# HGRN2 levels 4 and 8 from one set of keys: four 192-column matmuls in place of eight of 64 columns, and one yield fewer

## The chip, the cores and the metric

The kernel runs on one core of a Trainium2 chip. The metric is device microseconds of one execution; the kernel before takes 2802.47 us (median of 3 runs, 2801.3 to 2804.57). TensorE is PE in the rows below, VectorE is DVE, ScalarE is ACT and SyncE (which issues the DMAs) is SP.

## What is computed

One step of one decoder layer, for a prompt of 16 meta tokens and 256 tokens and for 8 single sample tokens, in float32:

```
x <- LN1(alpha*x + 0.5*SwiGLU_1(x))
x <- LN2(alpha*x + Mixer(x))        # retention (8 heads of 256) and HGRN2 (16 heads of 128)
x <- LN3(alpha*x + 0.5*SwiGLU_2(x))
```

In the mixer one projection `x @ w_in` gives ten parts of 2048 columns. The change lies in HGRN2, whose chunk is

```
b = cumsum(logf);  decay[i,j] = exp(b[i] - b[j]) for j <= i, else 0
A = einsum('bhid,bhjd,bhijd->bhij', q, k, decay)
o = A @ v + (q * exp(b)) @ S;   S_new = exp(b_last) * S + (k * exp(b_last - b))^T @ v
```

and every head's output is divided by the root of its mean square (`head_rms_norm`) before the gates.

## The kernel before, in words

**Dense stream.** All weights come as units of 512 KB, 8 blocks of 128x128. For each unit SP issues one load into `raw` (L158), ACT rounds it into `whi` (L161) and DVE subtracts to get the rest `wlo` (L162). `raw`, `whi` and `wlo` have three buffers each, so ACT can start `whi` of unit n only when PE has done its last matmul of unit n-3. PE multiplies each block three times (L191: `whi` by `xh`, `whi` by `xl`, `wlo` by `xh`), 24 matmuls per unit. I count units from the kernel's start, and "396.0" is the place on PE ahead of the first matmul of unit 396.

**Mixer.** Two column chunks are projected at a time, 16 k-steps each, so 4 k-steps use up one unit. After each k-step `pump` lets every waiting thread count down; a thread that has counted out runs on to its next `yield n` and then counts n k-steps. There are two kinds of thread: `mix_ret` (one for each of 8 retention heads) and `mix_hg` (one for each of 8 pairs u = 0 to 7 of HGRN2 heads). So PE's order is written by hand: the threads' small matmuls stand between dense matmuls, at a place that the sums of the yields decide. The other engines' order comes from a scheduler, in which the weight loads have high priority; it is fixed when the kernel is built, and each engine takes its instructions strictly in that order.

**mix_hg.** The decayed scores of a 128-token block are built by levels s = 1, 2, 4, ..., 64. At level s, `Q` holds queries with the decay since the start of their s-chunk, `K` keys with the decay to the end of theirs. Scores between an odd chunk's queries and the even chunk's keys ahead of it go into a PSUM bank `pl` (levels 4, 8 and 16 with L698: for each of two heads and two blocks all 128 keys by the block's 64 odd queries). DVE copies what a mask selects into `acch` (L734), multiplies the even keys and odd queries by their chunk's factor (L205 `K`, L205 `Q`) and yields 6 k-steps (8 after level 1). Levels 1 and 2 come from sums of products over the partitions (L202). After the levels, for each head h: transposes of K (`ptk`, L745), the sample states (`smh`: load L752, ACT L754, DVE L755), the state (`pst`), the sample queries (`pq`, L776), the output (`po`, L785 and L786). Then the square of `po` is split into `hhi` (ACT, L196) and `hlo` (DVE, L197), and 7 k-steps later PE adds it up over the partitions, `pv` (L202, once with `hhi` and once with `hlo`). `mix_ret` has the same kind of sum, `pvr` with `rhi` and `rlo`, its own scores `psc` (L848), states `psr` (L864), sample queries `pqr` (L894), and DVE updates of the sample states, `smr` (L885).

Banks of all these small groups (`mx_bank`) rotate through four.

Of the kernel before, what the change touches and what calls it, by code (L numbers as in the profile page):

```python
# [10 lines left out]
F32 = mybir.dt.float32  # L11
F32R = mybir.dt.float32r
U8 = mybir.dt.uint8
AF = mybir.ActivationFunctionType
ALU = mybir.AluOpType
# [3 lines left out]
P = 128  # L19
# [4 lines left out]
NMETA, SEQ, NS = 16, 256, 8  # L24
# [17 lines left out]
LEVELS = (1, 2, 4, 8, 16, 32, 64)  # L42
MASKED = 5

MASKS = {1: [0], 2: [1, MASKED], 4: [2], 8: [3], 16: [4]}
W_LEVEL = 6


# [53 lines left out]
def trunk(ctx: ExitStack, tc: tile.TileContext, A, O):  # L102
    nc = tc.nc
    cst = ctx.enter_context(tc.tile_pool(name="cst", bufs=1))
# [11 lines left out]
    def mx_bank(name):  # L116
        return ps_m.tile([P, 512], F32, tag="mx", name=name)
# [10 lines left out]
    lb = cst.tile([P, KC], F32, tag="lb", name="lb")  # L128
    olb = cst.tile([P, KC], F32, tag="olb", name="olb")
    dec = cst.tile([P, 3, HR], F32, tag="dec", name="dec")  # L130
    msk = cst.tile([P, MASKED + 1, 2 * P], U8, tag="msk", name="msk")
    lnb = cst.tile([P, 2, 2, KC], F32R, tag="lnb", name="lnb")
    nc.vector.memset(ones, 1.0)
    nc.scalar.copy(ones_r, ones)
# [69 lines left out]
    def mul(out, a, b):  # L204
        nc.vector.tensor_tensor(out=out, in0=a, in1=b, op=ALU.mult)  # L205
# [4 lines left out]
    def sub(out, a, b):  # L210
        nc.vector.tensor_tensor(out=out, in0=a, in1=b, op=ALU.subtract)
# [17 lines left out]
    def x_tiles(c, which, n=T):  # L229
        for e, (x, nm) in enumerate(((xh, "xh"), (xl, "xl"))):  # L230
            o = 4 * ((2 * c + e) // 8 % 2) + 8 * (c % 2) * e
            x[c] = xp.tile([P, XP], F32R, tag=f"{nm}{c}", name=f"{nm}{which}_{c}")[:, o : o + n]
# [206 lines left out]
    with tc.tile_pool(name="inp", bufs=2) as ip:  # L439
        def tokens(queue, c0, c1):  # L440
            x0 = ip.tile([P, c1 - c0, T], F32, tag=f"x0{c0}", name=f"x0{c0}", bufs=1)
            queue.dma_start(x0, A["x"][:, c0:c1, :])
            for c in range(c0, c1):
                x_tiles(c, 0)
                split(xh[c], xl[c], x0[:, c - c0, :])


        pw = mx_bank("pw")
        for _ in range(WARM):
            nc.tensor.matmul(pw[:, :P], ones, ones, start=True, stop=True)  # L450
        for c in range(2):
            with turn(2 * c):
                tokens(nc.scalar, c, c + 1)
        for c in range(2, KC, 2):
            with turn(c + 1):
                tokens(nc.sync, c, c + 2)
        mf = ip.tile([P, MASKED + 1, 2 * P], F32, tag="mf", name="mf", bufs=1)
        nc.sync.dma_start(mf[:, :MASKED, :], A["msk"])

        even = ip.tile([P, 1], F32, tag="even", name="even", bufs=1)  # L460
        nc.vector.tensor_reduce(out=even, in_=mf[:, 0, :], op=ALU.max, axis=mybir.AxisListType.X)
        nc.vector.tensor_copy(mf[:, MASKED, :], mf[:, 1, :])
        nc.vector.tensor_scalar(out=mf[:, 1, :], in0=mf[:, 1, :], scalar1=even, scalar2=None, op0=ALU.mult)
        sub(mf[:, MASKED, :], mf[:, MASKED, :], mf[:, 1, :])
        nc.vector.tensor_copy(msk, mf)
    nc.sync.dma_start(lnp, A["lnp"])
    nc.sync.dma_start(lbt, A["lb"])
# [7 lines left out]
    with tc.tile_pool(name="yp", bufs=1) as yp:  # L475
        yh, yl = [None] * KC, [None] * KC
        with tc.tile_pool(name="mp", bufs=1) as mp:
# [7 lines left out]
            def tmp(name, shape=(P, T), bufs=1, dt=F32, tag=None):  # L485
                if name in rows:
                    rows[name] = rows[name][1:] + rows[name][:1]
                    return rp.tile(list(shape), dt, tag=rows[name][-1], name=name)
                return mp.tile(list(shape), dt, tag=tag or name, name=name, bufs=bufs)
# [148 lines left out]
            def mix_hg(u, f, k, q, v):  # L638

                Q = tmp("Q", (P, 2, SEQ))  # L640
                K = tmp("K", (P, 2, LP))
# [8 lines left out]
                acc = tmp("acch", (P, 2 * SEQ))  # L650
# [11 lines left out]
                for h in range(2):  # L662
# [12 lines left out]
                    out=acc.rearrange("p (b c) -> p b c", b=4), in0=pd.rearrange("p (b c) -> p b c", b=4),  # L675
                    in1=ident.unsqueeze(1).to_broadcast([P, 4, P]), op=ALU.mult)
                Tt = f
                for s in LEVELS:
                    pl = mx_bank("pl")
                    if s == 1:  # L680
                        sums(pl[:, :SEQ], hilo, 2)
                    elif s == 2:
                        sums(pl.rearrange("p (i c) -> p i c", i=2), hilo)
                    for h in range(2 if s > 2 else 0):
                        for b in range(2):
                            k0, q0, o = NMETA + b * P, b * P, (2 * h + b) * min(s, 64)
                            if s == 64:
                                nc.tensor.matmul(
                                    pl[0:s, o : o + s], K[:, h, k0 : k0 + s], Q[:, h, q0 + s : q0 + 2 * s],
                                    start=True, stop=True)  # L690
                            elif s == 32:
                                for j in (0, 64):
                                    nc.tensor.matmul(
                                        pl[j : j + s, o : o + s], K[:, h, k0 + j : k0 + j + s],
                                        Q[:, h, q0 + j + s : q0 + j + 2 * s], start=True, stop=True, tile_position=(0, j))
                            else:
                                o = (2 * h + b) * 64
                                nc.tensor.matmul(  # L698
                                    pl[:, o : o + 64], K[:, h, k0 : k0 + P],
                                    Q[:, h, q0 : q0 + P].rearrange("p (n t s) -> p n t s", t=2, s=s)[:, :, 1, :],  # L700
                                    start=True, stop=True)

                    if s == NMETA:
                        Tt = Tt[:, :, 1:]
                    k0 = 0 if s < NMETA else NMETA
                    n = LP - k0
                    nb = n // s
                    m = nb // 2
                    t2 = Tt[:, :, :nb].rearrange("p h (n t) -> p h n t", t=2)
                    kv = K[:, :, k0:].rearrange("p h (n t s) -> p h n t s", t=2, s=s)  # L710
                    qv = Q.rearrange("p h (n t s) -> p h n t s", t=2, s=s)
                    mq = SEQ // (2 * s)
                    mul(kv[:, :, :, 0, :], kv[:, :, :, 0, :], t2[:, :, :, 1].unsqueeze(3).to_broadcast([P, 2, m, s]))
                    mul(qv[:, :, :, 1, :], qv[:, :, :, 1, :], t2[:, :, m - mq :, 0].unsqueeze(3).to_broadcast([P, 2, mq, s]))
                    Tn = tmp(f"T{2 * s}", (P, 2, m))
                    mul(Tn, t2[:, :, :, 0], t2[:, :, :, 1])
                    Tt = Tn
                    if s == 1:

                        q4 = Q.rearrange("p h (n t i) -> p h n t i", t=2, i=2)[:, :, :, 1, :]  # L720
                        hilo = [tmp("prod" + t, (P, 2, SEQ), dt=F32R, tag=t) for t in ("smh", "vbh")]
                        for j in range(2):
                            pr = tmp(f"pr{j}", (P, SEQ))
                            mul(pr.rearrange("p (h n i) -> p h n i", h=2, i=2), q4,
                                K[:, :, NMETA + j :: 4].unsqueeze(3).to_broadcast([P, 2, SEQ // 4, 2]))
                            split(hilo[0][:, j], hilo[1][:, j], pr)
                    if s >= 32:
                        for j in range(0, 128 // s, 2):
                            nc.scalar.copy(
                                acc[j * s : (j + 1) * s, :].rearrange("p (x n s) -> p x n s", x=4, s=s)[:, :, j + 1, :],  # L730
                                pl[j * s : (j + 1) * s, : 4 * s].rearrange("p (x s) -> p x s", x=4))
                    else:
                        for j, mi in enumerate(MASKS[s]):
                            nc.vector.copy_predicated(  # L734
                                acc.rearrange("p (n t s) -> p n t s", t=2, s=s)[:, :, 1, :],
                                msk[:, mi, :].rearrange("p (n s) -> p n s", s=s),
                                pl[:, j * SEQ : (j + 1) * SEQ].rearrange("p (n s) -> p n s", s=s))
                    yield W_LEVEL + 2 * (s == 1)
                on = tmp("on_h", (P, 2, TL), bufs=2)
                on_h[u] = on  # L740
                for h in range(2):
# [11 lines left out]
                    for b in range(NS):  # L753
                        nc.scalar.activation(sm[:, b, :], sm[:, b, :], AF.Copy, scale=fk[:, 0, h, b : b + 1])  # L754
                        nc.vector.scalar_tensor_tensor(  # L755
                            out=sm[:, b, :], in0=vb[:, b, :], scalar=fk[:, 1, h, b : b + 1], in1=sm[:, b, :],
                            op0=ALU.mult, op1=ALU.add)
# [9 lines left out]
                    for b in range(2):  # L767
                        nc.vector.scalar_tensor_tensor(
                            out=S[:, b + 1, :], in0=S[:, b, :], scalar=Tt[:, h, b : b + 1],
# [4 lines left out]
                    for b in range(NS):  # L774
# [3 lines left out]
                            start=b < 4, stop=b >= 4, tile_position=(0, j))  # L778
# [278 lines left out]
```

## Time and profile before

| what | value |
|---|---|
| median of 3 runs | 2802.47 us |
| profiled execution: time, span | 2802.12 us, 2800.2 us |
| PE busy | 2790.4 us (100%) |
| DVE busy, ACT busy | 1719.7 us (61%), 1353.0 us (48%) |
| TensorE clock granted, mean | 1.000 |
| mixer stage in the span | about 812 to 1890 us |

Busy times overlap between engines. The profile is of one execution; a row of the timeline gives start, duration, engine, line, operation and tiles. A PE row "x8" are eight records drawn together; a float32 matmul leaves two records, a matmul of the rounded type one.

### The profile page before, as it was taken

The numbers are of one execution on the slowest core, as the hardware profiler recorded it, in microseconds if no ns is written. First come the engines' busy times: TensorE is split into PE (matmuls) and PEld (weight loads), VectorE is DVE, ScalarE is ACT, GpSimd is POOL, SyncE is SP. The second block draws the span as 40 slices with busy tenths as digits, with TensorE's granted clock in tenths as the row PEclk, the third lists the DMA queues.
The fourth block names the chain that finished last, engine by engine and source line by source line (L and its number), as shares of the span: only waits on it lengthen the run. The fifth ranks groups of instructions, "written<-read, shape, count | busy, mean of one in ns | idle before, by whom it ended". The sixth has DMA issues, their size and how long they took to land.

```text
span 2800.2 us, 54485 instructions
## 1 busy us (share of the span) xinstructions
PE 2790.4 (100%) x22672; PEld 2760.1 (99%) x22672; DVE 1719.7 (61%) x2842; ACT 1353.0 (48%) x2033; POOL 4.3 (0%) x42
## 2 busy tenths in 40 slices
PE   9999999999999999999999999999999999999999
PEld 9999999999999999999999999999999999999998
DVE  5444444464479777777777777775884444446444
ACT  5434344333355564646464646464554444444333
POOL 0000000000000000000000000000000000000000
PEclk9999999999999999999999999999999999999999
DMA  6455554555556675757575657575555555555553
GB/s 231 168 173 171 170 173 169 171 171 168 173 173 219 200 257 183 245 182 247 182 244 184 246 181 248 179 244 180 181 176 182 182 183 182 181 181 181 181 179 139
DMA packets 154583, 536.26 MB, mean 192 GB/s; under 512 B 17696, under 2 KB 25696, under 8 KB 154336
## 3 DMA queue, kind: packets, MB, share of 16 engines
q1 hardware_dynamic: 154048, 532.50, 56.1%
q8 instruction: 177, 2.90, 0.4%
q14 instruction: 70, 0.57, 0.1%
q10 hardware_dynamic: 288, 0.29, 0.0%
HBM read 502.12 MB, written 30.61 MB: 190 GB/s over the span
## 4 chain that ended last, share of the span: by engine, by line
PE 98%; ACT 0%; DVE 0%; DMA 0%; issue 0%; SPq 0%; DVEq 0%
PE up L191 37%; PE dn L191 18%; PE pj_v_r L191 4%; PE pj_f L191 4%; PE pj_k_r L191 4%; PE pj_i_h L191 4%; PE pj_g_r L191 3%; PE pj_q_h L191 3%; PE wo L191 3%; PE pj_a_r L191 3%; PE pj_g_h L191 3%; PE pj_a_h L191 3%; PE pj_q_r L191 3%; PE pl L698 1%; PE pqr L894 1%; PE psr L864 0%
## 5 line engine op out<-in xcount | busy, mean ns | idle before, releaser
L162 DVE TENSOR_TENSOR wlo<-raw,whi 128x1024 fp32r<-128x1024 f32 (+1 forms) x869 | 1062.0, 1222 | 884.1 <-ACT whi L161 881.3
L161 ACT CAST whi<-raw 128x1024 fp32r<-128x1024 f32 (+1 forms) x870 | 909.3, 1045 | 1149.0 <-PE up L191 482.7
L191 PE MATMUL up<-xl,whi 128*128 128x280 f32 (+1 forms) x2688 | 765.4, 288 | 0.0
L191 PE MATMUL up<-xh,wlo 128*128 128x280 f32 (+1 forms) x2688 | 765.1, 288 | 0.0
L191 PE MATMUL up<-xh,whi 128*128 128x280 f32 (+1 forms) x2688 | 764.4, 287 | 0.1
L191 PEld LDWEIGHTS up<-xh,whi 128*128 128x128 f32 x2688 | 502.9, 188 | 0.3 <-ACT whi L161 0.3
L191 PEld LDWEIGHTS up<-xh,wlo 128*128 128x128 f32 x2688 | 502.9, 188 | 0.2 <-DVE wlo L162 0.2
L191 PEld LDWEIGHTS up<-xl,whi 128*128 128x128 f32 x2688 | 502.7, 188 | 0.0
L191 PE MATMUL dn<-hh,whi 128*128 128x280 f32 (+1 forms) x1376 | 397.1, 289 | 0.0
L191 PE MATMUL dn<-hl,whi 128*128 128x280 f32 (+1 forms) x1376 | 395.8, 288 | 0.0
L191 PE MATMUL dn<-hh,wlo 128*128 128x280 f32 (+1 forms) x1376 | 395.7, 288 | 0.0
L191 PEld LDWEIGHTS dn<-hl,whi 128*128 128x128 f32 x1376 | 259.0, 188 | 0.1
L191 PEld LDWEIGHTS dn<-hh,whi 128*128 128x128 f32 x1376 | 258.9, 188 | 0.1
L191 PEld LDWEIGHTS dn<-hh,wlo 128*128 128x128 f32 x1376 | 258.7, 188 | 0.0
L191 PE MATMUL pj_g_r<-xh,whi 128*128 128x264 f32 x256 | 78.9, 308 | 0.0
L191 PE MATMUL pj_v_r<-xh,whi 128*128 128x280 f32 x256 | 76.2, 298 | 0.0
L191 PE MATMUL pj_g_h<-xh,whi 128*128 128x264 f32 x256 | 75.9, 296 | 0.0
L191 PE MATMUL pj_k_r<-xh,whi 128*128 128x280 f32 x256 | 75.5, 295 | 0.0
L191 PE MATMUL pj_i_h<-xh,whi 128*128 128x280 f32 x256 | 74.9, 293 | 0.0
L191 PE MATMUL pj_v_r<-xl,whi 128*128 128x280 f32 x256 | 74.7, 292 | 0.0
L191 PE MATMUL pj_k_r<-xl,whi 128*128 128x280 f32 x256 | 74.6, 291 | 0.0
L191 PE MATMUL pj_i_h<-xl,whi 128*128 128x280 f32 x256 | 74.6, 291 | 0.0
(358 smaller groups left out, 5212.7 us busy)
## 6 DMA issues: line engine op xcount, KB each, us to landing
raw<-in_w_up SPq DMA_DIRECT2D x343, 512.0 KB, 3.4
raw<-in_w_in SPq DMA_DIRECT2D x320, 512.0 KB, 3.6
raw<-in_w_dn SPq DMA_DIRECT2D x172, 512.0 KB, 3.4
smr<-in_sr SPq DMA_DIRECT2D x32, 512.0 KB, 5.1
out_srs<-smr SPq DMA_DIRECT2D x32, 512.0 KB, 4.0
raw<-in_w_out SPq DMA_DIRECT2D x32, 512.0 KB, 3.4
smh<-in_sg SPq DMA_DIRECT2D x16, 512.0 KB, 3.4
out_sgs<-smh SPq DMA_DIRECT2D x16, 512.0 KB, 4.2
```

Source lines behind the costliest of these rows:

```text
L161: nc.scalar.copy(hi[:, j:jn, :], raw[:, j:jn, :])
L162: nc.vector.tensor_tensor(out=lo[:, j0:j1, :], in0=raw[:, j0:j1, :], in1=hi[:, j0:j1, :].bitcast(F32), op=ALU.subtract)
L191: nc.tensor.matmul(o, w, t, start=start, stop=stop)
L698: nc.tensor.matmul(pl[:, o : o + 64], K[:, h, k0 : k0 + P], Q[:, h, q0 : q0 + P].rearrange("p (n t s) -> p n t s", t=2, s=s)[:, :, 1, :], ...
L894: nc.tensor.matmul(pq[32 * j : 32 * j + 32, :256], qdr[:, c, 32 * b : 32 * b + 32], sms[c][:, j, :], start=c == 0, stop=c == 1, tile_posit ...
```

## The change

Keys scaled to the end of their 4-chunk serve two levels: for level 8, the keys of the earlier 4-chunk lack one factor, which is put on a copy of the queries instead. After level 2 a tile `Qm` of three times 256 columns is made (tag `smh`): the odd 4-chunk queries, the odd 8-chunk queries, and the odd 8-chunk queries times the factor of the 4-chunk between (two ACT copies, one DVE multiply). At s = 4, one PSUM bank per head takes two matmuls of 192 columns (64 of each kind), and three predicated copies of 128 columns per head put them into `acch`, with masks for level 4, for level 8's later and level 8's earlier keys. The L698 matmuls of levels 4 and 8 go, and their two predicated copies. The multiply of `Q` at level 4 moves ahead, into level 2. The mask of level 8 is split in two at the start. Level 2's yield grows from 6 to 8, level 4's yield goes.

```
-                    pl = mx_bank("pl")
+                    if s == 4:
+                        for h in range(2):
+                            pl = mx_bank("pl")
+                            for b in range(2):
+                                nc.tensor.matmul(
+                                    pl[:, 192 * b : 192 * b + 192], K[:, h, NMETA + b * P : NMETA + b * P + P],
+                                    Qm.rearrange("p i (x c) -> p i x c", x=4)[:, :, 2 * h + b, :], start=True, stop=True)
+                            for i, (sl, mi) in enumerate(((4, MASKS[4][0]), (8, MASKS[8][0]), (8, MASKS[8][1]))):
+                                nc.vector.copy_predicated(
+                                    acc[:, 2 * P * h : 2 * P * (h + 1)].rearrange("p (b n t s) -> p b n t s", b=2, t=2, s=sl)[:, :, :, 1, :],
+                                    msk[:, mi, :P].rearrange("p (b n s) -> p b n s", b=2, s=sl),
+                                    pl[:, :384].rearrange("p (b i n s) -> p b i n s", b=2, i=3, s=sl)[:, :, i])
+                    elif s != 8:
+                        pl = mx_bank("pl")
...
-                    for h in range(2 if s > 2 else 0):
+                    for h in range(2 if s > 8 else 0):
...
-                    mul(qv[:, :, :, 1, :], qv[:, :, :, 1, :], t2[:, :, m - mq :, 0].unsqueeze(3).to_broadcast([P, 2, mq, s]))
+                    if s != 4:
+                        mul(qv[:, :, :, 1, :], qv[:, :, :, 1, :], t2[:, :, m - mq :, 0].unsqueeze(3).to_broadcast([P, 2, mq, s]))
...
-                    if s >= 32:
+                    if s == 2:
+                        Qm = tmp("Qm", (P, 3, 2 * P), tag="smh")
+                        qf = Q.rearrange("p h c -> p (h c)")
+                        odd = [qf.rearrange("p (n t s) -> p n t s", t=2, s=sl)[:, :, 1, :] for sl in (4, 8)]
+                        nc.scalar.copy(Qm[:, 0, :].rearrange("p (n s) -> p n s", s=4), odd[0])
...
+                        mul(q4, q4, t4.unsqueeze(3).to_broadcast([P, 2, 32, 4]))
+                        nc.scalar.copy(Qm[:, 1, :].rearrange("p (n s) -> p n s", s=8), odd[1])
...
+                        mul(Qm[:, 2, :].rearrange("p (h n s) -> p h n s", h=2, s=8),
+                            Q.rearrange("p h (n t s) -> p h n t s", t=2, s=8)[:, :, :, 1, :],
+                            t4.unsqueeze(3).to_broadcast([P, 2, 16, 8]))
+                    if s in (4, 8):
+                        pass
+                    elif s >= 32:
...
-                    yield W_LEVEL + 2 * (s == 1)
+                    if s != 4:
+                        yield W_LEVEL + 2 * (s <= 2)
```

The yields from the start of the levels to a head's end sum to 4 k-steps fewer than before, one unit, so in every thread of HGRN2 all that follows level 4 stands a unit earlier on PE, while `mix_ret`'s groups stay where they are. Three places show it. Line numbers of the changed kernel are 7 larger up to the levels and 40 larger behind them.

First, PE in thread u = 3 where head 0's mean square is summed. Before, unit 396's last matmuls stand ahead of it (`_14981` and `_14982` are unit 396's `whi` and `wlo`), with `mix_ret`'s `pqr` in their middle:

```order
L894 MATMUL pqr<-smr,qdr 32x256 x8
L191 MATMUL pj_g_r_14892<-xh_11_8966,whi_14981 128x264
L191 MATMUL pj_g_r_14892<-xl_11_8967,whi_14981 128x264
L191 MATMUL pj_g_r_14892<-xh_11_8966,wlo_14982 128x264
L191 MATMUL pj_a_r_14893<-xh_11_8966,whi_14981 128x264
L191 MATMUL pj_a_r_14893<-xl_11_8967,whi_14981 128x264
L191 MATMUL pj_a_r_14893<-xh_11_8966,wlo_14982 128x264
L202 MATMUL pv<-hhi,ones_r 128x264
L202 MATMUL pv<-hlo,ones_r 128x264
L745 MATMUL ptk<-ident,K 128x128 x2
```

Now it is unit 395 whose last matmuls stand ahead of it (`_14971` and `_14972`), and unit 396 (`_15041`) comes behind it:

```order
L191 MATMUL pj_g_r_14923<-xl_7_8947,whi_14971 128x264
L191 MATMUL pj_g_r_14923<-xh_7_8946,wlo_14972 128x264
L191 MATMUL pj_a_r_14924<-xh_7_8946,whi_14971 128x264
L191 MATMUL pj_a_r_14924<-xl_7_8947,whi_14971 128x264
L191 MATMUL pj_a_r_14924<-xh_7_8946,wlo_14972 128x264
L202 MATMUL pv<-hhi,ones_r 128x264
L202 MATMUL pv<-hlo,ones_r 128x264
L785 MATMUL ptk<-ident,K 128x128 x2
L785 MATMUL ptk<-ident,K 16x128
L191 MATMUL pj_g_r_14923<-xh_8_8952,whi_15041 128x264
```

The pair of sums has moved from 397.0 to 396.0; threads u = 4 to 7 read alike, 40 units apart.

Second, DVE at the same place. Before, `wlo` of units 396, 397 and 398 are `_14982`, `_15066` and `_15107`:

```order
L162 TENSOR_TENSOR wlo_14982<-raw_14980,whi_14981 128x8x128
L205 TENSOR_TENSOR gt<-gt,gs 128x264
L885 SCALAR_TENSOR_TENSOR smr<-vbr,k_r,smr 128x256 x4
L612 SCALAR_TENSOR_TENSOR gt<-gt,ngt,on_h 128x264
L162 TENSOR_TENSOR wlo_15066<-raw_15064,whi_15065 128x8x128
L885 SCALAR_TENSOR_TENSOR smr<-vbr,k_r,smr 128x256 x4
L208 TENSOR_TENSOR y<-y,gt 128x264
L635 COPY on_h<-po 128x8
L205 TENSOR_TENSOR sqh<-on_h 128x8
L162 TENSOR_TENSOR wlo_15107<-raw_15105,whi_15106 128x8x128
L197 TENSOR_TENSOR yl_14889<-y,yh_14888 128x264
L197 TENSOR_TENSOR hlo<-sqh,hhi 128x264
```

Now the same three are `_15042`, `_15086` and `_15127`; the first row below follows `wlo_15042`, and `smr` x4 and `gt` between them:

```order
L642 COPY on_h<-po 128x8
L619 SCALAR_TENSOR_TENSOR gt<-gt,ngt,on_h 128x264
L205 TENSOR_TENSOR sqh<-on_h 128x8
L208 TENSOR_TENSOR y<-y,gt 128x264
L925 SCALAR_TENSOR_TENSOR smr<-vbr,k_r,smr 128x256 x3
L162 TENSOR_TENSOR wlo_15086<-raw_15084,whi_15085 128x8x128
L925 SCALAR_TENSOR_TENSOR smr<-vbr,k_r,smr 128x256
L197 TENSOR_TENSOR yl_14920<-y,yh_14919 128x264
L162 TENSOR_TENSOR wlo_15127<-raw_15125,whi_15126 128x8x128
L197 TENSOR_TENSOR hlo<-sqh,hhi 128x264
L795 SCALAR_TENSOR_TENSOR smh<-vbh,fk,smh 128x128 x7
```

Head 0's first steps on DVE (`on_h`, `sqh`) have moved up by about a unit, but `hlo` still stands behind the `wlo` of unit 398.

Third, DVE in thread u = 1, where `mix_ret` scales its keys for the state (`ks`, from the transposed keys `pt`; three scalings read each bank of them, and the 24-partition one is the last). On PE at 308.25 `psc` takes, in the changed kernel, the bank of the first of these `pt`. Before, the third row of `ks` here is the 24-partition one, ahead of `wlo` of unit 310 (`_11120`):

```order
L211 TENSOR_TENSOR vs_8630<-vt_8627,vs_8630 24x128
L205 TENSOR_TENSOR K<-K,T_10864 128x68x4
L837 SCALAR_TENSOR_TENSOR ks_8629<-pt,dec,ks_8629 24x128
L205 TENSOR_TENSOR Q<-Q,T_10864 128x64x4
L734 COPY_PREDICATED acch<-msk,pl 128x64x4
L162 TENSOR_TENSOR wlo_11120<-raw_11118,whi_11119 128x8x128
L837 SCALAR_TENSOR_TENSOR ks<-pt,dec,ks 128x128
```

Now it stands behind `wlo` of unit 310 (`_11142`):

```order
L211 TENSOR_TENSOR vs_8634<-vt_8631,vs_8634 24x128
L877 SCALAR_TENSOR_TENSOR ks<-pt,dec,ks 128x128
L846 TENSOR_SCALAR cen<-cen 128x2
L847 TENSOR_TENSOR vtr<-vtr,cen 128x512
L162 TENSOR_TENSOR wlo_11142<-raw_11140,whi_11141 128x8x128
L877 SCALAR_TENSOR_TENSOR ks_8633<-pt,dec,ks_8633 24x128
L877 SCALAR_TENSOR_TENSOR ks<-pt,dec,ks 128x128
L696 COPY_PREDICATED acch<-msk,pl 128x32x4 x2
```

On PE of the changed kernel the fused matmuls, `psc` and the dense stream stand there as `L692 MATMUL pl<-Qm,K 128x192 x4`, then L888 `psc`, then unit 308's dense matmuls.

More of the change, by code (lines that the diff above doesn't have):

```diff
@@ L43 @@
 MASKED = 5
-MASKS = {1: [0], 2: [1, MASKED], 4: [2], 8: [3], 16: [4]}
+MASKS = {1: [0], 2: [1, MASKED], 4: [2], 8: [3, MASKED + 1], 16: [4]}
 W_LEVEL = 6
@@ L130, in trunk @@
     dec = cst.tile([P, 3, HR], F32, tag="dec", name="dec")
-    msk = cst.tile([P, MASKED + 1, 2 * P], U8, tag="msk", name="msk")
+    msk = cst.tile([P, MASKED + 2, 2 * P], U8, tag="msk", name="msk")
     lnb = cst.tile([P, 2, 2, KC], F32R, tag="lnb", name="lnb")
@@ L456, in trunk @@
                 tokens(nc.sync, c, c + 2)
-        mf = ip.tile([P, MASKED + 1, 2 * P], F32, tag="mf", name="mf", bufs=1)
+        mf = ip.tile([P, MASKED + 2, 2 * P], F32, tag="mf", name="mf", bufs=1)
         nc.sync.dma_start(mf[:, :MASKED, :], A["msk"])
[L460 to L464, printed above, removed]
+        for i, mi in enumerate((1, 3)):
+            part = ip.tile([P, 1], F32, tag=f"part{i}", name="part", bufs=1)
+            nc.vector.tensor_reduce(out=part, in_=mf[:, mi - 1, :], op=ALU.max, axis=mybir.AxisListType.X)
+            own, end = mf[:, mi, :], mf[:, MASKED + i, :]
+            if i == 0:
+                nc.vector.tensor_copy(end, own)
+                nc.vector.tensor_scalar(out=own, in0=own, scalar1=part, scalar2=None, op0=ALU.mult)
+                sub(end, end, own)
+            else:
+                nc.vector.tensor_scalar(out=end, in0=own, scalar1=part, scalar2=None, op0=ALU.mult)
+                sub(own, own, end)
         nc.vector.tensor_copy(msk, mf)
@@ L726, in mix_hg @@
                             split(hilo[0][:, j], hilo[1][:, j], pr)
-                    if s >= 32:
+                    if s == 2:
[3 more added lines that the diff above has]
+                        nc.scalar.copy(Qm[:, 0, :].rearrange("p (n s) -> p n s", s=4), odd[0])
+                        t4 = Tt[:, :, NMETA // 4 :].rearrange("p h (n t) -> p h n t", t=2)[:, :, :, 0]
+                        q4 = Q.rearrange("p h (n t s) -> p h n t s", t=2, s=4)[:, :, :, 1, :]
+                        mul(q4, q4, t4.unsqueeze(3).to_broadcast([P, 2, 32, 4]))
+                        nc.scalar.copy(Qm[:, 1, :].rearrange("p (n s) -> p n s", s=8), odd[1])
+                        t4 = Tt[:, :, NMETA // 4 :].rearrange("p h (n t) -> p h n t", t=4)[:, :, :, 1]
+                        mul(Qm[:, 2, :].rearrange("p (h n s) -> p h n s", h=2, s=8),
[4 more added lines that the diff above has]
+                    elif s >= 32:
                         for j in range(0, 128 // s, 2):
```

## The prediction

> **What bounds the kernel now.** The page's span, its busy times and the chain that ended last come first.
>
> ```profile
> span 2800.2 us, 54485 instructions
> PE 2790.4 (100%) x22672; PEld 2760.1 (99%) x22672; DVE 1719.7 (61%) x2842; ACT 1353.0 (48%) x2033; POOL 4.3 (0%) x42
> PE 98%; ACT 0%; DVE 0%; DMA 0%; issue 0%; SPq 0%; DVEq 0%
> L162 DVE TENSOR_TENSOR wlo<-raw,whi 128x1024 fp32r<-128x1024 f32 (+1 forms) x869 | 1062.0, 1222 | 884.1 <-ACT whi L161 881.3
> ```
>
> PE is never idle; the other engines idle a third of the time or more, DVE nearly always waiting for `whi`, that is for PE to free a weight buffer. So a PE matmul less is time won, and DVE or ACT work costs nothing as long as PE doesn't wait for it. The waits of PE show how often it does:
>
> ```profile
> engine line waited for: us in total, times, longest us
> PE pvr L202 <- DVE rlo L197: 1.2, 1, 1.2
> PE pl L693 <- DVE Q L205: 1.2, 1, 1.2
> PE pw L450 <- DVE eps_h L136: 1.0, 1, 1.0
> ```
>
> Two waits in the whole mixer. The yields place every small group just late enough. That makes a shortened sum of yields the thing to look at, beside the saved matmuls.
>
> **The matmuls.** Two stretches of PE's timeline give a level group and a `psc` group, and the groups by form give single durations:
>
> ```profile
> 878.11 1.00 PE L698 MATMUL pl<-Q,K 128*128 128x64 f32 x8
> 878.92 0.37 PE L191 MATMUL pj_v_r<-xh,whi 128*128 128x280 f32 x1
> 879.13 0.29 PE L191 MATMUL pj_v_r<-xl,whi 128*128 128x280 f32 x1
> 879.26 0.29 PE L191 MATMUL pj_v_r<-xh,wlo 128*128 128x280 f32 x1
> ...
> 892.15 1.71 PE L848 MATMUL psc<-q_r,k_r 128*128 128x256 f32 x12
> 893.79 0.40 PE L191 MATMUL pj_f<-xh,whi 128*128 128x280 f32 x1
> ```
>
> A level group is four float32 matmuls, eight records. The next dense matmul starts 0.81 us later and the one behind it after 0.21 us, where 0.13 is usual (879.13 to 879.26): 0.81 + 0.08 = 0.89 us per group. Eight records in 0.81 us are 0.10 each: 64 columns don't set the time, something fixed does. The twelve records of `psc`, four each of 256, 144 and 16 columns, take 1.64 us; with 0.10 for each of the last four, 1.24 are left for 4 x (256 + 144) = 1600 columns, 0.78 ns a column, a little under what the dense rows would give for two passes over the columns (0.13 for 280 is one pass, 0.93 for two). By the two, a 192-column record takes 0.15 to 0.18 us; I take 0.162, between them. Eight of them are 1.30 us, and since they stream longer than a fixed 0.10 I expect no slow start behind them.
>
> Removed: 2 groups x 8 threads x 0.89 = 14.2 us. Added: 8 x 1.30 = 10.4 us. Net **-3.9 us**. Bounds: at the floor of 0.10 the added work is 6.5 us, net -7.7; at the 0.20 of a 256-column record (0.78 ns a column) 12.8, net -1.4. Six level-4 groups had a transposing group as neighbour and shared its slow start; alone, that group pays up to 0.08 more: **+0.3 us**.
>
> **DVE, ACT and the rest.**
>
> ```profile
> L734 DVE COPY_PREDICATED acch<-msk,pl 128x256 f32<-128x256 uint8 x48 | 27.9, 582 | 0.3
> L205 DVE TENSOR_TENSOR Q<-Q,T 128x256 f32<-128x256 f32 x48 | 20.0, 417 | 0.0
> ```
>
> Per thread two copies of 582 ns become six of half the columns (0.3 each if time goes by columns, 0.58 if it doesn't), one 0.42 multiply comes for `Qm`, and ACT gets two copies of about 0.4: at most 2.8 us more DVE work in a thread that lasts over 100 us. DVE's 39% idle time hides it, so I cost it at 0; without that cover it would be 8 x 2.8 = 22 us at most. `Qm` has a level's wait of 8 k-steps, two units, to be made in. The masks at the start are a few DVE operations beside the first FFN: 0. `smh` now holds `Qm` until the fused matmuls are done, so the load of the sample states starts later but still well before `pq`, over four units on: 0.
>
> **What moves.** With 4 k-steps fewer, everything behind level 4 comes one unit earlier against the retention thread and against what feeds it. For the levels, the transposes and `po` I find that the operands are ready a microsecond or more ahead. The sum `pv` of head 0 is where I don't. The timeline at its place in thread u = 3 before, 397.0:
>
> ```profile
> 1301.66 0.28 PE L191 MATMUL pj_a_r<-xh,wlo 128*128 128x264 f32 x1
> 1301.86 1.05 ACT L161 CAST whi<-raw 128x1024 fp32r<-128x1024 f32 x1 [1.92 <-PE pj_a_r L191]
> 1302.94 1.23 DVE L162 TENSOR_TENSOR wlo<-raw,whi 128x1024 fp32r<-128x1024 f32 x1 [0.50 <-ACT whi L161]
> ...
> 1304.08 0.43 DVE L197 TENSOR_TENSOR yl<-y,yh 128x264 fp32r<-128x264 f32 x1
> ...
> 1304.42 0.43 DVE L197 TENSOR_TENSOR hlo<-sqh,hhi 128x264 fp32r<-128x264 f32 x1
> ...
> 1305.89 0.29 PE L202 MATMUL pv<-hhi,ones_r 128*128 128x264 f32 x1
> ...
> 1306.02 0.29 PE L202 MATMUL pv<-hlo,ones_r 128*128 128x264 f32 x1
> ```
>
> The matmul at 1301.66 is the last of unit 395; it frees a buffer, ACT makes `whi` of unit 398 from it at 1301.86, DVE its `wlo` at 1302.94, and `hlo` comes behind that, done at 1304.85. `pv` needs it at 1306.02: 1.17 us to spare. Now `pv` stands directly behind unit 395's last matmul, a unit (24 matmuls, 2.9 us) and a `pqr` group (about 1 us) earlier, while on DVE `hlo` still stands behind `wlo` of unit 398, as the rows of the change show. DVE takes its instructions in order, so PE waits, behind the last matmul of unit 395, for `whi`, `wlo` and `hlo`. With S the start of that matmul: `whi` from S + 0.20, `wlo` from S + 1.28, `hlo` (no `yl` between now) from S + 2.42 to S + 2.85. The second `pv` would have started at S + 0.24. Stall: at least 2.85 + 0.05 - 0.24 = **2.66 us**.
>
> DVE may be later still. Between the start of unit 396's `wlo` and the end of `hlo` there are now three `wlo` (1.14 us from start to start), eight `smr`, and eight short ones.
>
> ```profile
> 1300.54 1.27 DVE L885 SCALAR_TENSOR_TENSOR smr<-vbr,k_r,smr 128x256 f32<-128x256 f32 x3
> 1301.73 0.43 DVE L208 TENSOR_TENSOR y<-y,gt 128x264 f32<-128x264 f32 x1
> 1302.07 0.16 DVE L635 COPY on_h<-po 128x8 f32<-128x8 f32 x1
> 1302.27 0.17 DVE L205 TENSOR_TENSOR sqh<-on_h 128x8 f32<-128x8 f32 x1
> L612 DVE SCALAR_TENSOR_TENSOR gt<-gt,ngt,on_h 128x264 f32<-128x264 f32 x16 | 7.8, 490 | 0.3
> ```
>
> ```profile
> 1298.58 0.39 PE L785 MATMUL po<-acch,vth 128*128 128x128 f32 x2
> ...
> 1299.47 0.27 PE L634 MATMUL po<-ident,osh 128*128 128x128 f32 x1
> ```
>
> Three `smr` take 1.19 from start to start of what follows, `y` and its like 0.34, the tiny ones 0.2: 3.4 + 3.2 + (0.34 + 0.2 + 0.45 + 0.15 + 0.35 + 0.34) + 0.43 = 8.8 us. PE, from the moment at which that first `wlo` can start to the second `pv`, has units 394 and 395 and the `po` group (the two rows, 0.9 and the way in) less 1.28: 5.8 + 1.0 + 0.24 - 1.28 = 5.8 us. That gives a stall of 3.0, and 3.9 if durations are taken whole instead of starts. I take 3.1. Threads u = 3 to 7 have this order: 5 x 3.1 = **+15.5 us** (13.3 to 19.5). In thread u = 2 `hlo` stands ahead of that `wlo`, but DVE has as much in hand: 7.3 us of work against 5.8, at most 1.5; by the buffer alone 0.4. I take **+1.0**. Threads 0 and 1, and head 1 everywhere, have one and a half units between, more than 2.85 us.
>
> What is queued behind: on PE the transposes of head 1 and the dense stream, so the stall is lost whole; the dense matmuls behind aren't slower or faster for it, and DVE and ACT get ahead by 3 us, so nothing else is late there.
>
> Before shows the same chain once, in the retention's `pvr`:
>
> ```profile
> 942.04 0.39 PE L202 MATMUL pvr<-rhi,ones_r 128*128 128x264 f32 x1
> 942.06 1.22 DVE L162 TENSOR_TENSOR wlo<-raw,whi 128x1024 fp32r<-128x1024 f32 x1
> 943.19 0.42 DVE L197 TENSOR_TENSOR rlo<-sqr,rhi 128x264 fp32r<-128x264 f32 x1
> 943.67 0.39 PE L202 MATMUL pvr<-rlo,ones_r 128*128 128x264 f32 x1 [1.24 <-DVE rlo L197]
> 943.90 0.28 PE L191 MATMUL pj_q_r<-xh,whi 128*128 128x264 f32 x1
> 944.02 0.28 PE L191 MATMUL pj_q_r<-xl,whi 128*128 128x264 f32 x1
> ```
>
> `rlo` behind a `wlo`, PE late by 943.67 - 942.16 = 1.5 us. This wait and the one of 1.2 at L693 are in threads 0 and 1, whose groups also move by a unit; a `pst` group now fills most of the first, and the second level 32 has more ahead of it. I take both as gone: **-2.7 us** (0 to -2.7). New in thread 1: `psc` waits for `ks` behind `wlo` of unit 310, by the same count E + 2.85 after unit 307 ends, against six dense matmuls and the fused group, 2.0: **+1.3 us** (0.8 to 2).
>
> **Sum.** -3.9 + 0.3 + 15.5 + 1.0 - 2.7 + 1.3 = **+11.5 us**, 0.41%. On the profiled execution's 2802.12 that is 2813.6; the median stands 0.35 higher, so 2814.
>
> **Rivals.** (A) Faster: the new waits don't come and only the saved matmuls and the two waits of before are left. `pv` at 396.0 is free to start once `hlo` is made, and the data for `hlo` (`po` at 394.25, `sqh`, `hhi`) are there in time; if `hlo` were done before unit 398's `wlo`, no stall of `pv` would be left: -3.9 + 0.3 - 2.7 = -6.3, 2796. It is decided by which of the two DVE takes first. For it: before, nothing was lost at any `pv`. Against: the order of the rows, which the chip can't change. With part of the waits (under 9 us in all) the time is within 0.2%, which is about what a measurement of this kernel can tell from no change: 2802.
>
> (B) Deeper: DVE also waits for the sample states' loads, two `smr` more (0.8 us) ahead of `hlo` each time, in six threads: 0.8 x 6 + 4 = +9 on top, 2823. For it: eight `smr` stand there now. Against: loads are issued long ahead.
>
> (C) The idle PE loses its clock. In before the dense matmuls after the idle 1.24 us at 943.67 go on at 0.12 us apart, and the granted clock of the run is 1.000, so a stall of 1.5 us cost only itself. If 3 us were over a limit, and half the clock were granted for as long as the stall, 5 x 1.5 = +8 us: 2822. The Trainium skill, "TensorE: Matmul & The Clock Gate", section "HAM oscillation — how this bites in real kernels", states such a limit: an idle gap over about 3.4 us drops the array to half its clock. The stalls I expect lie just under that figure and the trace of before has none so long, so it can't say.
>
> **How the numbers follow.** Forecast, five stalls near 3 us: 0.70, 2806 (13.3 of stalls and the fused records at the floor) to 2822. A faster 0.06, A in part 0.12, B 0.06, C 0.06. The range that leaves out 2 in 10: 2800 to 2824. Faster 0.06, same 0.13 (with a little of the forecast's low end), slower 0.81.
>
> **What would show it.** In the waits of PE: `pv` L202 on DVE `hlo`, five or six times, 15 to 18 us in all, longest 3 to 4; the `pvr` wait gone. In the timeline at each of 396.0, 436.0, ...: ACT `whi`, DVE `wlo`, `hlo`, then `pv`, with no gap. The fused group at 1.3 us. DVE near 62% of the span, `wlo` ahead of the dense stream everywhere else. I'm wrong if `pv` doesn't wait, or if fused records take much other than 0.16.

## The result and the profile after

The changed kernel takes 2837.63 us (median of 4 runs, 2836.25 to 2841.45) against 2801.93 us of the kernel before in all its runs up to then: ratio 1.0127, 95% interval 1.0115 to 1.0139. That is 36 us slower, where 12 were forecast and 2824 was the upper end of the range. The profiled execution's span is 2834.5 us, 34.3 more than before.

Of the page, the span, the busy times and the chain:

```profile
span 2834.5 us, 54421 instructions
PE 2800.6 (99%) x22608; PEld 2765.9 (98%) x22608; DVE 1726.3 (61%) x2885; ACT 1361.4 (48%) x2049; POOL 4.3 (0%) x42
PE 94%; DMA 2%; DVE 2%; ACT 1%; issue 0%; SPq 0%; DVEq 0%; ACTq 0%
```

PE has 64 instructions fewer and is busy 10 us longer: its instructions have become slower, not only later. In the chain 5% are DMA, DVE and ACT, which had none before; by line, the DMA share is the load of `smr`. The waits of PE (us in total, times, longest us) name the place:

```profile
PE pv L202 <- DVE hlo L197: 13.2, 6, 2.6
PE pv L202 <- ACT hhi L196: 10.6, 6, 3.4
PE psc L888 <- DVE ks L877: 1.3, 1, 1.3
PE pw L450 <- DVE eps_h L136: 1.0, 1, 1.0
PE pvr L202 <- DVE rlo L197: 0.9, 1, 0.9
PE up L191 <- ACT whi L161: 0.5, 1, 0.5
```

Six waits at `pv`, as forecast, in threads 2 to 7; but each comes in two parts. `hhi`, which I had taken to be ready, is late too. The timeline at 396.0 in thread 3, to be read beside the prediction's S + 0.20, S + 1.28, S + 2.42:

```profile
1301.73 1.07 ACT L922 ACTIVATE smr<-smr 128x1024 f32<-128x1024 f32 x1 [1.21 <-DMA smr<-in_sr]
1302.70 1.03 ACT L161 CAST whi<-raw 128x1024 fp32r<-128x1024 f32 x1
...
1303.32 0.28 PE L191 MATMUL pj_a_r<-xh,wlo 128*128 128x264 f32 x1
1303.64 0.41 ACT L196 CAST yh<-y 128x264 fp32r<-128x264 f32 x1
1303.95 0.38 ACT L829 ACTIVATE sqh<-po 128x256 f32<-128x256 f32 x1
...
1304.48 0.41 ACT L196 CAST hhi<-sqh 128x264 fp32r<-128x264 f32 x1
1304.79 1.05 ACT L161 CAST whi<-raw 128x1024 fp32r<-128x1024 f32 x1
1304.94 0.39 PE L202 MATMUL pv<-hhi,ones_r 128*128 128x264 f32 x1 [1.34 <-ACT hhi L196]
...
1306.27 1.22 DVE L162 TENSOR_TENSOR wlo<-raw,whi 128x1024 fp32r<-128x1024 f32 x1
1307.41 0.43 DVE L197 TENSOR_TENSOR hlo<-sqh,hhi 128x264 fp32r<-128x264 f32 x1
...
1307.89 0.39 PE L202 MATMUL pv<-hlo,ones_r 128*128 128x264 f32 x1 [2.55 <-DVE hlo L197]
1308.12 0.50 PE L785 MATMUL ptk<-ident,K 128*128 128x128 f32 x3
1308.36 0.48 PE L191 MATMUL pj_g_r<-xh,whi 128*128 128x264 f32 x1
1308.63 0.42 PE L191 MATMUL pj_g_r<-xl,whi 128*128 128x264 f32 x1
1308.85 0.42 PE L191 MATMUL pj_g_r<-xh,wlo 128*128 128x264 f32 x1
```

S is 1303.32, and unit 398's `whi` starts at S + 1.47, its `wlo` at S + 2.95, `hlo` at S + 4.09. ACT is the late one: the second `smr` waited for its load (the bracket: 1.21 us), `whi` of unit 397 came behind it, then `yh`, the square, `on_h`, `hhi`, and only then unit 398's `whi`. From where the second `pv` would have stood to where it stands, threads 2 to 7 lose 2.35, 4.33, 6.05, 5.18, 5.06 and 3.56 us, 26.5 in all. That is more than the 23.8 us of waits in the view because the view counts a wait from the end of the matmul ahead, and here it is counted from start to start.

And the dense matmuls behind it are 0.22 us apart, not 0.12. The same stretches by windows (of each row the third number from the end is the granted clock):

```profile
core 0: us, PE busy (x) PEld busy (x) DVE busy (x) ACT busy (x) POOL busy (x), PEclk, DMA share, GB/s
1305.00:1308.00 3.00, 0.45 (x2) 0.24 (x2) 3.00 (x6) 2.90 (x8) 0.00 (x0) 1.00 0.36 42
1308.50:1311.80 3.30, 3.30 (x17) 3.30 (x17) 2.10 (x8) 2.73 (x6) 0.00 (x0) 0.50 1.00 385
1312.00:1315.00 3.00, 3.00 (x33) 2.27 (x32) 1.60 (x6) 0.83 (x1) 0.00 (x0) 1.00 0.43 176
1448.50:1451.80 3.30, 1.38 (x12) 1.17 (x10) 2.22 (x8) 1.68 (x2) 0.00 (x0) 1.00 0.53 211
1451.90:1455.20 3.30, 0.59 (x1) 0.29 (x1) 3.30 (x6) 3.30 (x10) 0.00 (x0) 0.50 0.43 36
1455.30:1458.60 3.30, 2.71 (x12) 2.63 (x13) 2.38 (x9) 2.85 (x7) 0.00 (x0) 0.50 0.81 299
1458.70:1462.00 3.30, 3.30 (x23) 2.60 (x26) 1.47 (x4) 1.05 (x4) 0.00 (x0) 0.50 0.53 217
1462.10:1465.00 2.90, 2.90 (x28) 2.50 (x21) 1.75 (x5) 1.56 (x2) 0.00 (x0) 1.00 0.19 78
```

After the wait in thread 3 the clock is 0.50 for 3.41 us, after the longer one in thread 4 for 10.24 us; in thread 5 for 6.83, in 6 and 7 for 3.41 each. Dense matmuls that follow one another lose some 6.8 us to it, and the `pv`, transposes and a `pqr` group in those stretches about 2.9 more: 9.7.

The sum of the 34.3: waits at `pv` 26.5, half clock 9.7, the new wait of `psc` 1.6; less 3.9 for the matmuls, 1.2 for the wait at level 32 and 0.4 of the one at `pvr`; 0.3 for the lost neighbours. That is 32.6; 1.7 us are spread over groups and not assigned.

### The profile page after: what moved, and what is told of

It is laid out like the page before. It is cut to its first block, busy times and chain, and to the rows that moved or that the text cites. A ratio compares the mean times of both kernels' runs of the same rounds, so it can differ in the third digit from the quotient of the medians.

```text
span 2834.5 us, 54421 instructions
## 1 busy us (share of the span) xinstructions
PE 2800.6 (99%) x22608; PEld 2765.9 (98%) x22608; DVE 1726.3 (61%) x2885; ACT 1361.4 (48%) x2049; POOL 4.3 (0%) x42
## 4 chain that ended last, share of the span: by engine, by line
PE 94%; DMA 2%; DVE 2%; ACT 1%; issue 0%; SPq 0%; DVEq 0%; ACTq 0%
PE up L191 36%; PE dn L191 18%; PE pj_f L191 4%; PE pj_v_r L191 4%; PE pj_k_r L191 3%; PE pj_i_h L191 3%; PE pj_q_h L191 3%; PE wo L191 3%; PE pj_q_r L191 3%; PE pj_g_r L191 3%; PE pj_a_r L191 3%; PE pj_g_h L191 3%; PE pj_a_h L191 3%; DMA smr<-in_sr 2%; DVE wlo L162 1%; DVE smr L925 1%
```

## The experiments

Theory 1: the place of `pv`, one unit earlier, is the cause of the loss. Theory 2: idle PE loses the clock, which is a cost of its own. Rival: the fused matmuls, `Qm` or the narrower copies cost. How a loss of 4.4 us a thread (the mean of the six) came about where 3 was forecast needed two theories more.

**The wait put back (e1).** Four more k-steps after level 8; fused matmuls stay.

```
-                        yield W_LEVEL + 2 * (s <= 2)
+                        yield W_LEVEL + 2 * (s <= 2) + 4 * (s == 8)
```

> The changed kernel with four more k-steps yielded after level 8, so that all that follows stands where it stood before; the fused matmuls stay. If the place of the sums pv is what costs (theory 1): no wait of PE at pv, granted clock 1.000, and only the saved matmuls are left, 2802 - 4 = 2798 (2797 to 2800). If the fused matmuls, Qm or the half-width copies cost (rival): 2815 or more, with PE waiting elsewhere.

Measured 2801.6 us (11 runs), ratio 0.9997 (0.9989 to 1.0006), clock 1.000. Its waits:

```profile
PE psc L888 <- DVE ks L877: 1.3, 1, 1.3
PE pvr L202 <- DVE rlo L197: 1.2, 1, 1.2
PE pw L450 <- DVE eps_h L136: 1.0, 1, 1.0
PE pqr L934 <- DVE smr L925: 0.9, 1, 0.9
PE pl L715 <- DVE Q L205: 0.7, 1, 0.7
```

No wait at `pv`: the rival falls and the 36 us are the yield's. But 2798 was missed by 3.6, and the range (2797 to 2800) with it: two waits, `psc` and `pqr` in threads 0 and 1, are new and take back 2.2 us of the 3.9.

**The yield alone (e2).** The kernel before, with head 0's four k-steps taken out ahead of `pst`.

```
-                    yield 14 if u else 8
+                    yield (14 if u else 8) - 4 * (h == 0)
```

> The kernel before with head 0's wait ahead of pst shortened by four k-steps and nothing else: levels and transposes of head 0 as before, all behind them a unit earlier. Theory 1 (the place of pv): the same waits at pv as in the changed kernel, 22 to 27 us, clock 0.995 or so, time 2802 + 24 + 10 + 3 = 2839 (2833 to 2844). Rival (the fused part costs): about 2802.

Measured 2841.12 us, ratio 1.0133 (1.0119 to 1.0147), clock 0.995; waits at `pv` 13.5 (`hlo`) and 12.3 us (`hhi`). The changed kernel's loss without its matmuls. Theory 1 stands, from both sides.

**PE kept busy (e5).** The stretches of waiting in threads 3 to 7 filled with matmuls that nobody reads, 6 to 26 ahead of the first `pv` and 16 between the two.

```
+                    n0 = {3: 10, 4: 26, 5: 18, 6: 17, 7: 6}.get(u, 0) if h == 0 else 0
+                    for _ in range(n0):
+                        nc.tensor.matmul(pv[:, TL : TL + 248], ones_r, xh[0][:, :248], start=True, stop=True)
...
+                    for _ in range(16 if n0 else 0):
+                        nc.tensor.matmul(pv[:, TL : TL + 248], ones_r, xh[0][:, :248], start=False, stop=False)
```

> The changed kernel with 157 extra matmuls of 248 columns in the stretches in which PE waits at pv (threads 3 to 7), into columns of the bank that nobody reads: work added, nothing taken away. If idle PE is what lowers the clock (theory 2): clock 1.000 and 2837 - 10 = 2827 (2824 to 2831), faster with more work. If the clock falls for another reason: 2837 or more, clock 0.995.

Measured 2828.51 us (2827.78 to 2829.28), clock 0.999: 9.1 us faster than the changed kernel by 157 more matmuls. In threads 3 to 7 the clock holds; it falls once, in thread 2, which has no filling and kept its clock in the changed kernel. A stretch of e5 in thread 4, at the time at which the changed kernel was at half clock, and the one behind thread 2's wait (the third number from the end is the clock):

```profile
1451.90:1455.20 3.30, 3.30 (x29) 3.13 (x28) 3.30 (x9) 3.25 (x10) 0.00 (x0) 1.00 0.45 96
1162.90:1166.20 3.30, 3.30 (x17) 3.28 (x15) 2.05 (x6) 3.24 (x8) 0.00 (x0) 0.50 0.94 307
```

Theory 2 stands, and the half clock was worth 9 us or a little more.

**`hlo` ahead of `wlo` (e4).**

```
-                    split(*hilo, sq)
+                    with tc.high_priority():
+                        split(*hilo, sq)
```

> The changed kernel with the split into hhi and hlo at high priority, which puts hlo ahead of the wlo of unit 398 on DVE; PE's order is the same. If the order on DVE is the cause of the second wait: the wait at hlo, 13.2 us, falls to 3 or less, the one at hhi (10.6) stays, less clock is lost: 2816 to 2824. If DVE and ACT simply have too much in hand there: 2832 or more.

Measured 2823.21 us, ratio 1.0071 (1.0056 to 1.0087), clock 0.997:

```profile
PE pv L202 <- ACT hhi L196: 10.5, 6, 2.5
PE pv L202 <- DVE hlo L197: 3.2, 6, 0.7
```

The part at `hlo` was DVE's order, as predicted: 13.2 to 3.2 us with PE's order untouched. The part at `hhi` stays.

**Theory 3: the load of `smh` (e6, e9, and with e4's priority e8, e10).** In the changed kernel head 1's load of `smh` goes out 0.7 us behind the second load of `smr` (before: 9.5 us behind), and ACT's waits for `smr` rise from 16.1 to 36.5 us. I took the one for the cause of the other. e6 asks for the load four k-steps later:

```
+                    yield 4
                     vb = tmp("vbh", (P, NS, P))
...
-                    yield 14 if u else 8
+                    yield (14 if u else 8) - 4
```

> The changed kernel with the loads of vbh and smh (sample states) and the work on them four k-steps later, pst where it was. Theory 3: the load of smh, issued 7 us earlier than before, slows the load of smr, which holds up ACT ahead of whi and hhi. Then PE's wait for hhi falls from 10.6 us to 5 or less, that for hlo (order on DVE) stays at 12 to 15: 2824 to 2832. If the loads don't matter: hhi 9 to 12, 2835 or more.

> e4 (hlo ahead of the wlo) and e6 (load later) together, pv where the change puts it. If order and load are the two parts of the wait: both waits at 5 us or less, clock 1.000 or nearly, 2802 - 1 + 8 = 2809 (2805 to 2813). If one of them covers the other: like e4, 2823.

e6 measured 2836.48 us (waits 14.0 for `hhi` and 12.9 for `hlo`), e8, with the priority as well, 2823.83 (9.5 and 3.8). But the load still went out 0.7 us behind that of `smr`: it goes as soon as `pq` has freed the tile (in thread 3 of e6 `pq` ends at 1298.84 and the load goes out at 1298.91), wherever it is asked for. So e6 and e8 say nothing of the theory, and e9 holds the load back with a dependence:

```
+                    if h == 1:
+                        nc.gpsimd.tensor_copy(out=sm[:, 0, 0:1], in_=sq[:, 0:1])
                     nc.sync.dma_start(sm, A["sg"][2 * u + h])
```

> The changed kernel with one GpSimd copy of a column of head 0's squares into the tile that head 1's smh load fills, so that this load can only go out once the squares are made (in e6 it still went out 0.7 us behind the second load of smr). Theory 3: without that load beside it, the load of smr lands sooner, ACT waits less for it, and PE's wait at hhi falls from 10.6 us to 5 or less; the wait at hlo, which is order on DVE, stays at 12 to 15: 2822 to 2830. If the load beside it doesn't matter: hhi 9 to 12, 2834 or more.

> e9 with e4's priority for the split (hlo ahead of the wlo). If load and order are the two parts: both waits at 5 us or less, clock 1.000, 2804 to 2813. If the load doesn't matter: like e4, 2819 to 2825.

Now it goes out 11 us behind (1297.9 and 1309.0 in thread 3), and e9 takes 2840.62 us, waits for `hhi` 11.1 us, ACT's for `smr` 40.8. e10: 2817.48 us, waits 7.1 and 3.6, and a new one of 2.5 at `por`. Theory 3 falls as the main cause: without the load beside it, `hhi` is as late as before. A small part stays open: e10 lies between its two forecasts (2804 to 2813, 2819 to 2825), 5.7 us below e4, and its wait for `hhi` is 7.1 us where e4 has 10.5.

**Theory 4: ACT's order (e13).** What remains is where the second `smr` stands on ACT. In the kernel before and in e1 it is behind `whi` of unit 397, and `hhi` comes later still; in e2, e4, e9, e10 and the changed kernel it is ahead of it, as the timeline of the changed kernel above shows (`smr` at 1301.73, `whi` of unit 397 at 1302.70, `hhi` at 1304.48). ACT of the kernel before, in thread 3, with `whi` of unit 397 first:

```profile
1297.92 1.05 ACT L161 CAST whi<-raw 128x1024 fp32r<-128x1024 f32 x1 [1.09 <-PE pj_a_r L191]
1298.88 1.06 ACT L882 ACTIVATE smr<-smr 128x1024 f32<-128x1024 f32 x1
...
1303.65 0.42 ACT L196 CAST hhi<-sqh 128x264 fp32r<-128x264 f32 x1
```

So in the changed kernel `whi` and `hhi` stand behind an instruction that waits for a 512 KB load. ACT's waiting for `smr` doesn't cost by itself: e1 has 26.2 us of it and no wait of PE at `pv`. e13 gives the whole way from `po` to the split high priority, so that the scheduler puts it ahead on ACT and on DVE:

```
+                    with tc.high_priority():
+                        sample_columns(on[:, h, :], po, os)
+                        sq = tmp("sqh", (P, TL))
+                        nc.scalar.activation(sq[:, :SEQ], po[:, :SEQ], AF.Square)
...
+                        split(*hilo, sq)
```

> The changed kernel with high priority for all of head 0's and head 1's way from po to hhi and hlo (squares and sample columns too). PE's order is the changed kernel's; on ACT hhi now stands ahead of the second smr, on DVE hlo ahead of the wlo of units 397 and 398. Theory 4: the wait at hhi comes from ACT's order, in which the scaling of smr waits for its load ahead of whi of unit 397 and hhi. Then both waits at pv fall to 2 us or less in all, clock 1.000, 2800 to 2806 (the waits of psc and others of the first threads stay). If ACT and DVE have too much in hand whatever their order: waits at pv of 8 us or more, 2812 or more.

Measured 2805.04 us (11 runs), ratio 1.0009 (0.9999 to 1.0018). Its timeline in thread 3 and its waits:

```profile
1299.30 0.38 ACT L830 ACTIVATE sqh<-po 128x256 f32<-128x256 f32 x1
1299.57 0.38 ACT L834 COPY on_h<-po 128x256 f32<-128x256 f32 x1
1299.82 0.43 ACT L196 CAST hhi<-sqh 128x264 fp32r<-128x264 f32 x1
1300.43 0.43 DVE L197 TENSOR_TENSOR hlo<-sqh,hhi 128x264 fp32r<-128x264 f32 x1
1300.88 1.06 ACT L923 ACTIVATE smr<-smr 128x1024 f32<-128x1024 f32 x1 [0.63 <-DMA smr<-in_sr]
```

```profile
PE por L641 <- DVE osr L848: 3.2, 4, 1.0
PE psc L889 <- DVE ks L878: 1.3, 1, 1.3
PE pw L450 <- DVE eps_h L136: 1.0, 1, 1.0
PE pvr L202 <- DVE rlo L197: 0.9, 1, 0.9
PE pqr L935 <- DVE smr L926: 0.4, 1, 0.4
PE pv L202 <- DVE hlo L197: 0.2, 1, 0.2
```

`hhi` is made ahead of the `smr` that still waits for its load, and of 23.8 us of waits at `pv` 0.2 are left, with PE's matmuls in the same order as in the changed kernel. ACT still waits 31.0 us for `smr`. So an early `pv` costs next to nothing by itself; the order in which ACT and DVE serve it does. e4 gives DVE's share of that (13.2 to 3.2 us at `hlo`); e13 puts ACT's right as well. A part has moved on: `osr` is now late for `por`, 3.2 us. In e13 the second `smr` still stands ahead of `whi` of unit 397; no run moves `smr` alone, and why the scheduler put it there isn't shown.

**`pv` alone put back (e3).**

```
-                    yield 14 if u else 8
+                    yield (14 if u else 8) - 4 * (h == 1)
...
-                    yield 7
+                    yield 7 + 4 * (h == 0)
```

> The changed kernel with only head 0's pv and the transposes behind it put back by four k-steps; levels, pst, pq, po and all of head 1 stay a unit early. If pv alone is the cause: no wait at pv of threads 3 to 7, clock 1.000, 2798 to 2803. If the other early groups also cost (their loads a unit early, head 1 included): 2806 or more with waits elsewhere.

Measured 2805.56 us (11 runs), ratio 1.0012 (1.0003 to 1.0021): 0.3 us of waits at `pv` left, but 1.3 at `psc`, 1.2 at `pst` (its transposes now stand four k-steps nearer in thread 0) and 1.0 at `pqr`. That is just outside both forecasts (2798 to 2803, 2806 or more), 4 us behind e1, and 32 ahead of the changed kernel: `pv` is where nearly all of it was lost. ACT has the second `smr` ahead of `whi` of unit 397 here too; with `pv` a unit later it costs almost nothing.

**A version that keeps the gain (e7).** e1, with its four waits moved away from:

```
-                        yield W_LEVEL + 2 * (s <= 2)
+                        yield W_LEVEL + 2 * (s <= 2) + 4 * (s == 8) + (u == 1) * ((s == 2) - (s == 8) + (s == 16) - (s == 32))
...
-                    yield 14
+                    yield 14 + (u == 0 and e == 1)
...
-                yield 7
+                yield 7 + 2 * (u == 0)
```

> e1 (four k-steps back after level 8) with the four waits that e1 still shows in threads 0 and 1 (psc 1.3, rlo 1.2, smr 0.9, Q of level 32 0.7 us) moved away from: in thread 1 one k-step more ahead of the fused group and of level 32, given back later; in the retention's thread 0 one more ahead of the second pqr and two more ahead of pvr. If these waits are where the rest of e1's gain went: 2801.6 - 4 = 2797.6 (2796.5 to 2799), no wait of PE left in the mixer. If not: about 2801.

Measured 2797.76 us (11 runs, 2796.63 to 2800.93) against 2802.12: ratio 0.9987, 0.9978 to 0.9996. Its waits:

```profile
PE pw L450 <- DVE eps_h L136: 1.0, 1, 1.0
PE pl L715 <- DVE Q L205: 0.6, 1, 0.6
PE pst L803 <- ACT km L787: 0.2, 1, 0.2
```

This is the fastest of the kernels here, 4.4 us ahead of the kernel before (by the interval, 1 to 6): of the 3.9 for the matmuls and the 2.1 us by which the two old waits are shorter, most is kept. The kernel before wasn't given such yields, so no run separates the two parts.

## Why the prediction was wrong

**The matmuls: right, in part by luck.** A fused group costs 1.299 us in the stream (forecast 1.30), 0.162 us a record. The way there was off: the 16-column records of `psc` take 0.03 us each, not 0.10, and those of 256 and 144 columns 0.215 and 0.122, which is 0.84 ns a column and not 0.78; the middle of two rates happened to hit it. DVE's copies of half width take 293 ns (forecast 0.3), all hidden.

**The place: right.** `pv` waits in threads 2 to 7, in the forecast order `whi`, `wlo`, `hlo`; nowhere else does the unit's shift cost much (e3: 4 us more than e1). `hlo` behind `wlo` is the cause of the second part of the wait (e4). Rival A fell with it.

**The failed step: "Stall: at least 2.66 us", taken as 3.1, "13.3 to 19.5" for five.** They measured 24.2, mean 4.8. The step let ACT start unit 398's `whi` at S + 0.20, because the matmul at S frees the buffer. But freeing the buffer is one condition, and ACT's turn is the other. ACT's order is as fixed as DVE's, and it had changed too: the second `smr`, which waits for its load, had come ahead of `whi` of unit 397. Of the 1.27 us by which unit 398's `whi` missed S + 0.20 in thread 3, 1.21 are that wait by the timeline; that the same order held up `hhi`, and so the first part of the wait, e13 shows. The step added up DVE's work and took ACT as free; a busy share of 48% says nothing of a wait within a fixed order. Rival B had this (`smr` waiting for a load), but on DVE and with 0.8 us a thread.

**The second failed step: "the dense matmuls behind aren't slower or faster for it".** They ran at half clock, 9 to 10 us in all (e5: 9.1). Rival C, at 0.06 and +8, was right that idle PE loses the clock. That its price is near is partly luck: it took the stretch at half clock to be as long as the stall, while the stretches are one to three times 3.41 us and the stalls were longer than forecast. The row that I weighed against it, the idle 1.24 us of before without loss, spoke only of waits that short.

**The small terms.** `psc` 1.6 (forecast 1.3). Thread 2: 2.35 (forecast 1.0). The two waits of before: 1.6 gone of the 2.7.

With 26.5 for the waits and 9.7 for the clock in place of 16.5 and 0, the sum comes to 31, near the measured 34.

## What to carry to other kernels

When a group on a static, hand-ordered engine is moved earlier, list for each engine that feeds it every instruction from the last known time to the operand, in that engine's new order, and look first for one that waits for a DMA: the whole queue waits with it. Waits that leave PE idle for some 2 us within 3.41 us are to be priced twice, once as idle time and once as a stretch at half clock behind it (in these runs; the next section has the figures). A fusion that saves little time per place should leave the places of everything else alone (e1), or the yields have to be set again for the new order (e7).

## What the runs showed of the hardware

The granted clock falls at fixed times. In every run with several falls, the times at which it falls and rises differ by whole multiples of 3.41 us: 1308.47 and 1602.01 in the changed kernel are 86 of them apart. Over the eight runs with waits at `pv`, taking PE's idle time between its records within each window of 3.41 us: every window with 1.9 us or more idle was followed by half clock, no window at full clock with less than 1.65 was, and between 1.65 and 1.9 both happened. Half clock lasted through whole windows, and ended behind a window with at most 0.12 us idle; behind one with 0.65 us idle it went on. So it isn't the length of one wait that counts but where it lies: thread 2 of the changed kernel, with 0.79 us ahead of the edge and 1.13 behind, kept its clock.

The Trainium skill, "TensorE: Matmul & The Clock Gate", section "What's actually happening", gives the same window, 3413 ns and free-running, and the trace agrees. The Trainium skill, "TensorE: Matmul & The Clock Gate", section "HAM oscillation — how this bites in real kernels", puts the limit at idle gaps over about 3.4 us. Here a single wait of 2.55 us in one window was enough (thread 3 of the changed kernel), and the measurement decides.

At half clock dense matmuls of 264 columns stand 0.22 us apart, against 0.12 at full clock: 1.8 times as long, not twice.
